# Attention steps of a two-layer fp32 trunk: loads issued one step ahead of their use, the samples' matmuls placed behind their step's scores

## The chip, the cores and the metric

One core of one Trainium2 chip runs the whole program. The metric is the device time of one execution in microseconds (us). The core has five engines that each run their own instructions in order: PE (TensorE: matmuls and transposes), DVE (VectorE), ACT (ScalarE), POOL (GpSimd) and SP (SyncE), which here only issues DMA transfers. An instruction that has to wait holds everything behind it on its own engine.

## The reference

One inference step of a trunk of two layers, each an attention and a gated feed-forward part with a causal convolution. It runs over 1024 prompt positions and over 8 samples of 16 new positions with caches, 1152 positions in all, with 1024 features, all in fp32. Layer 0 (mixer A) has 16 query heads on 4 key/value heads, a window of the own chunk of 64 and two before it, and a learned sink; layer 1 (mixer B) has 16 heads of keys and values shared from one projection, and a band of the own chunk and eight before it. Every part is conditioned (adaLN) by a vector c and closed by a LayerNorm of a scaled residual:

```python
ada = (sc @ w_ada[l] + b_ada[l])[:, None, :]          # sc = silu(c)
sh_m, sc_m, g_m, sh_f, sc_f, g_f = jnp.split(ada, 6, axis=-1)
h = x * (1 + sc_m) + sh_m
q = h @ w_q;  k, v = ...                              # layer 1: shared k_b, v_b
s = einsum(q, k) * ATTN_SCALE + bias;  s = where(valid, s, NEG_INF)
o = softmax(s, with sinks in layer 0) @ v
x = layer_norm(DEEPNORM_ALPHA * x + (1 + g_m) * (o @ w_o), ...)
h = x * (1 + sc_f) + sh_f
f = (gelu(conv(h @ w_up)[g]) * conv(h @ w_up)[a]) @ w_down
x = layer_norm(DEEPNORM_ALPHA * x + (1 + g_f) * f, ...)
```

## The kernel before, in words

The program runs an opening, tables, and then for each layer an attention, its output projection and a feed-forward part. An fp32 operand is split into a high part (a cast on ACT, L166) and a low part (a subtraction on POOL or DVE, L177), and a product takes three matmuls on the parts; `split` does both.

An attention is a loop of 64 steps: 8 groups of columns times 2 heads times 4 pairs of query tiles. A step issues the scores of its pair (`scores`: matmuls L548 and L551, then the softmax on DVE at L515 and ACT's exponential at L519). Around them the loop places, by tables that are indexed by the step number: the projection of later queries (`qload` and `qblock`, table QAT; PE L295), the row sums (`sums`, PE L624, a DMA at L627), the transposes of the weights of an earlier half (`weigh`: PE L576, the cast by ACT at L582, the subtraction by DVE at L583), the products with the values (`finish`: PE L598, ACT L611, DVE L612, POOL L636, the store to oN in DRAM at L638), and the samples' work (table ITEMS: `item_scores` L687, `item_weigh` L713 with its copies on DVE at L714 and L715, `item_values` L722 with DVE L730, `item_out` L735 with DVE L744). Towards the end of the loop the attention's outputs come back from oN and are split for the output projection (`oload`, table OAT, DMA L644, into H), the samples' outputs too (`sload`, SAT), and the first four tiles of the output projection's weights are loaded (`woload`, WAT, DMA L181). The output projection's matmuls are those at L308.

In the first attention there is also background work: `ada(1)` and `ada(2)` multiply c by 16 slabs of 512 KB of conditioning weights each. A slab is one DMA (L215), then four matmuls (L223), which the trace shows as eight. The loop calls `self.step(BGA)`, which moves this work on by 0.6 of a slab a step.

All of these loads of 512 KB (queries' weights, conditioning, outputs, output projection's weights) pass through `ws`, a ring of two staging slots: a load's DMA can go out when the slot's last reader is done, an ACT cast and a POOL subtraction, or PE for a slab of conditioning.

What stands where on an engine is set by a scheduler that walks the program and puts each instruction into its engine's order by a modelled time. `issue_after(m)` holds the instructions of its block behind instruction m on the same engine; it sets an order and makes nothing wait on another engine. Where `split` is called sets from when its cast may be put into ACT's order.

Of the kernel before, what the change touches and what calls it, by code (L numbers as in the profile page):

```python
# [102 lines left out]
class Trunk:  # L103
    def __init__(self, ctx, tc, I, O):
# [53 lines left out]
        self.items = []  # L158
# [20 lines left out]
    def wload(self, src, eh="a", el="p", dst=None):  # L179
# [3 lines left out]
        self.split(s, h, l, eh, el)  # L183
        self.step(self.bgrate)
        return h, l

# [19 lines left out]
    def ada(self, gi, bank, ring=None):  # L206
# [4 lines left out]
        lead = [None] * 4  # L211
        for k in range(8):
            for hf in range(2):
                w = ring.next()
                nc.sync.dma_start(w, self.I["adaw"][gi, k, hf])  # L215
                for j in range(4):
                    with ExitStack() as es:
                        if lead[j] is not None:
                            es.enter_context(self.tc.issue_after(lead[j]))
                        if j:  # L220
                            es.enter_context(self.tc.high_priority())
                            es.enter_context(self.tc.issue_after(first))
                        mm = nc.tensor.matmul(  # L223
                            ps[32 * j : 32 * j + 32, hf * 256 : hf * 256 + 256],
                            self.cT[:, k * 32 : k * 32 + 32],
                            w[:, j * 256 : j * 256 + 256],
                            start=k == 0 and hf == 0,
                            stop=k == 7 and hf == 1,
                            tile_position=(0, 32 * j),
                            skip_group_check=True,  # L230
                        )
                    first = mm.ins if j == 0 else first
                    lead[j] = lead[j] or mm.ins
                yield
# [140 lines left out]
    def attention(self, l, wk):  # L375
# [132 lines left out]
        def qload(c):  # L508
            qw[c] = self.wload(I[("wq0", "wq1")[l]][c])
# [1141 lines left out]
```

## Time and profile before

| | us |
|---|---|
| median of 3 runs | 2829.28 |
| lowest and highest | 2822.47, 2830.57 |
| profiled execution: its own time | 2830.02 |
| its span, first to last instruction | 2828.2 |
| PE busy | 2717.7 (96% of the span) |
| DVE busy | 1813.6 (64%) |
| ACT busy | 1294.3 (46%) |
| POOL busy | 1171.1 (41%) |
| mean granted TensorE clock | 0.986 |

Busy time of PE includes time at a lowered clock. The span less PE's busy time, 110.5 us, is the time in which PE did nothing. The first attention runs from about 105 to 395 us, the second from about 1545 to 1945 us; the feed-forward parts take most of the rest. In a row of waits stand the waiting line, what released it, the total in us, the number of times and the longest. In a row of windows stand the busy time (and the number of instructions) of each engine in the stretch, then the granted TensorE clock, the busy share of the DMA engines and their GB/s. In a row of the timeline stand the start and the duration in us, the engine, the line, the operation, the tiles, the shape and the number of like instructions taken together, and in brackets the idle time ahead of it with its releaser.

### The profile page before, as it was taken

To read this page: it belongs to the slowest core of one execution; us is meant where nothing else is said; L and a number is where in the kernel's file an instruction comes from. 1 tells how busy PE (TensorE), PEld (TensorE's weight loads), DVE (VectorE), ACT (ScalarE), POOL (GpSimd) and SP (SyncE) were. 2 spreads that over 40 slices of the span, in tenths; PEclk is the share of its full clock that TensorE was granted. 3 is DMA by queue.
4 is the path that set the end of the run, shared out by engine and by line. 5 is a ranking of instruction groups with operands and counts; after the bars stand their busy time and mean duration, and the time that the engine had idled before them with its cause. 6 is when DMAs were issued, how large, how long until landed. Compare 5 with 4: busy or idle time off the path is not lost. (4 is left out here: it accounts for less than half of the span.)

```text
span 2828.2 us, 47410 instructions
## 1 busy us (share of the span) xinstructions
PE 2717.7 (96%) x17734; PEld 2419.7 (86%) x17734; DVE 1813.6 (64%) x3673; ACT 1294.3 (46%) x2624; POOL 1171.1 (41%) x773
## 2 busy tenths in 40 slices
PE   7999999999999999999999899979999999999997
PEld 5887768989999998887999788857899999997886
DVE  4475768776666783565112767666787778874764
ACT  3475733433333443544325666662454444444442
POOL 2132433444443457664731121242454433358662
PEclk9999999999999999999999999999999999999999
DMA  8655444464444346664875457683532222247652
GB/s 296 217 159 178 124 150 163 150 234 144 145 146 152 134 148 219 231 216 163 289 243 186 115 142 194 173 254 105 174 122 80 74 74 78 71 138 250 211 198 80
DMA packets 214598, 468.00 MB, mean 165 GB/s; under 512 B 35456, under 2 KB 109904, under 8 KB 214368
## 3 DMA queue, kind: packets, MB, share of 16 engines
q1 hardware_dynamic: 214368, 464.98, 50.2%
q8 instruction: 139, 2.28, 0.3%
q14 instruction: 91, 0.75, 0.1%
HBM read 365.17 MB, written 109.17 MB: 168 GB/s over the span
## 5 line engine op out<-in xcount | busy, mean ns | idle before, releaser
L1227 PE MATMUL PS<-H,wh 128*128 128x256 f32 (+1 forms) x2560 | 395.9, 297 | 0.0
L1227 PEld LDWEIGHTS PS<-H,wh 128*128 128x128 f32 x2560 | 361.6, 191 | 0.4 <-issue 0.4
L1292 DVE TENSOR_TENSOR xa<-xa 128x384 fp32r<-128x384 f32 x132 | 182.5, 1393 | 222.9 <-ACT xa L166 221.3
L1189 DVE TENSOR_TENSOR F<-PS,F 128x192 f32<-128x192 f32 (+2 forms) x600 | 192.0, 350 | 180.0 <-PE PS L1227 176.9
L177 POOL TENSOR_TENSOR wl<-ws,wh 128x1024 fp32r<-128x1024 f32 x72 | 182.1, 2533 | 276.9 <-ACT wh L166 263.9
L295 PE MATMUL PS<-H,wh 128*128 128x384 f32 (+1 forms) x1536 | 294.7, 337 | 0.0
L166 ACT CAST wh<-F 128x512 fp32r<-128x512 f32 (+1 forms) x230 | 155.1, 681 | 296.2 <-PE PS L1227 150.5
L1066 DVE SCALAR_TENSOR_TENSOR F<-F 128x1024 f32<-128x1024 f32 x320 | 265.7, 871 | 4.8 <-ACT F L1105 3.4
L295 PEld LDWEIGHTS PS<-H,wh 128*128 128x128 f32 x1536 | 267.1, 188 | 1.4 <-issue 0.8
L1227 PE MATMUL PS<-H,wl 128*128 128x256 f32 (+1 forms) x1280 | 229.1, 299 | 9.2 <-ACT F L1194 5.1
L177 DVE TENSOR_TENSOR wl<-F,wh 128x512 fp32r<-128x512 f32 x198 | 197.9, 1007 | 44.2 <-ACT wh L166 43.6
L166 ACT CAST wh<-ws 128x512 fp32r<-128x512 f32 (+1 forms) x158 | 129.6, 825 | 207.7 <-PE PS L1227 89.7
L1299 PE MATMUL PS<-wh,xa 128*128 128x512 f32 x696 | 222.5, 396 | 0.0
L1227 PEld LDWEIGHTS PS<-H,wl 128*128 128x128 f32 x1280 | 189.9, 191 | 16.9 <-issue 6.2
L1227 PE MATMUL PS<-xa,wh 128*128 128x256 f32 (+1 forms) x1280 | 196.1, 295 | 0.5 <-DVE xa L177 0.5
L1227 PEld LDWEIGHTS PS<-xa,wh 128*128 128x128 f32 x1280 | 178.6, 188 | 1.3 <-DVE xa L177 0.9
L1075 POOL TENSOR_TENSOR F<-F 128x16 f32<-128x16 f32 x88 | 46.6, 530 | 312.4 <-DVE F L1066 230.6
L308 PE MATMUL PS<-wh,H 128*128 128x256 f32 (+1 forms) x936 | 171.0, 314 | 4.5 <-DVE X L364 3.0
L295 PE MATMUL PS<-H,wl 128*128 128x384 f32 (+1 forms) x768 | 154.7, 342 | 2.5 <-ACT H L166 2.1
L1299 PEld LDWEIGHTS PS<-wh,xa 128*128 128x128 f32 x696 | 130.6, 188 | 30.6
L166 ACT CAST xa<-xa 128x384 fp32r<-128x384 f32 x132 | 67.5, 513 | 186.5 <-DMA xa<-actD 186.4
L636 POOL TENSOR_TENSOR F<-F,X 64x512 f32<-64x512 f32 x62 | 80.3, 1295 | 171.1 <-DVE F L612 134.1
(255 smaller groups left out, 6119.9 us busy)
## 6 DMA issues: line engine op xcount, KB each, us to landing
F<-in_wdn_dram SPq DMA_DIRECT2D x72, 512.0 KB
ws<-in_adaw_dram SPq DMA_DIRECT2D x64, 512.0 KB
ws<-in_wdn_dram SPq DMA_DIRECT2D x60, 512.0 KB
actD<-F SPq DMA_DIRECT2D x44, 576.0 KB
xa<-actD SPq DMA_DIRECT2D x132, 192.0 KB
ws<-in_wup_dram SPq DMA_DIRECT2D x49, 512.0 KB
F<-in_adaw_dram SPq DMA_DIRECT2D x48, 512.0 KB
F<-in_wup_dram SPq DMA_DIRECT2D x39, 512.0 KB
```

The source lines that it names most:

```text
L166: nc.scalar.copy(out, in_)
L177: self.eng(el).tensor_sub(lo, src, hi.bitcast(F32))
L295: mm = self.nc.tensor.matmul(out[:, 0:n], w[a][:, k * 128 : k * 128 + 128], H[:, p, k, s0 : s0 + n], start=i == 0, stop=i == 23)
L308: self.nc.tensor.matmul(out[:, 0:n], H[:, p, j * kn + k, t0 : t0 + 128], w[a][:, k * n : k * n + n], start=i == 0, stop=i == 23,)
L636: self.eng("v" if last else "p").tensor_mul(on[r, q], on[r, q], rb[r, :])
L1066: nc.vector.scalar_tensor_tensor(o, u, cw[:, cc, i : i + 1], o, op0=ALU.mult, op1=ALU.add)
L1075: nc.gpsimd.tensor_add(y3[:, :, 0:2], y3[:, :, 0:2], E4[:, cc])
L1189: nc.vector.tensor_add(d, o, x)
L1227: self.pairmm = nc.tensor.matmul(ps[:, 0:m], w[a][:, k * 128 : k * 128 + 128], x(p, k, n), start=start and c == 0, stop=c == 11, skip_grou ...
L1292: nc.vector.tensor_sub(lo, raw, hi.bitcast(F32))
L1299: self.downmm = nc.tensor.matmul(ps, a[p][:, i * 128 : i * 128 + 128], w[q][:, hf * 512 : hf * 512 + 512], start=j == 0 and c == 0, stop=j ...
```

## The change

The loads of the two attentions are cut in two. The DMA is put out at one step, and the split (ACT's cast and the low part) goes on a list, `todo`, that is run just behind the scores of the next step, with its ACT part queued behind the last exponential of those scores (`amark`). This holds for the queries' weights from the second group on, the attention's outputs, the samples' outputs and the first four tiles of the output projection's weights. The queries' loads go out one step earlier (at step 8c-1), the last group's at 47 instead of 48; the outputs' loads one a step (steps 51 to 56, where two went out at 51 before), and the samples' outputs and the projection's weights one step later.

The conditioning of the first attention gets a ring of one slot of its own, `ws[1]`, and all other loads there have only `ws[0]` until it is done; then the ring of two is back. A slab's DMA goes out in one call of the generator and its matmuls come in the next, with the first of them queued behind the last score matmul so far (`pmark`). The rate BGA goes from 0.6 to 0.7 slabs a step.

Of the samples' work, the loads of a sample (`item_load`) are issued one sample ahead: the first ahead of the loop, the next behind the values of the one before. The PE part of each piece is queued behind the step's last score matmul.

The diff, cut to its core:

```diff
-BGA = 0.6
+BGA = 0.7
 BGF = 1.3
 QAT = {}
+for c in range(7):
+    QAT[max(0, 8 * c - 1)] = [(c + 1, None)]
 for c in range(5):
-    QAT[8 * c] = [(c + 1, None)]
     for j, k in enumerate((1, 3, 6)):
         QAT[8 * c + k] = [(c + 1, j)]
-QAT.update({40: [(6, None)], 41: [(6, 0)], 43: [(6, 1)], 46: [(6, 2)], 48: [(7, None), (7, 0)], 49: [(7, 1)], 50: [(7, 2)]})
-OAT = {51: (0, 1), 52: (2,), 53: (3,), 54: (4,), 55: (5,)}
-SAT = 56
-WAT = {57: 0, 58: 1, 59: 3, 60: 2}
+QAT.update({41: [(6, 0)], 43: [(6, 1)], 46: [(6, 2)], 48: [(7, 0)], 49: [(7, 1)], 50: [(7, 2)]})
+OAT = {51: 0, 52: 1, 53: 2, 54: 3, 55: 4, 56: 5}
+SAT = 57
+WAT = {58: 0, 59: 1, 60: 3, 61: 2}
...
-    def wload(self, src, eh="a", el="p", dst=None):
+    def wload(self, src, eh="a", el="p", dst=None, later=False):
         s = self.ws.next()
         self.nc.sync.dma_start(s, src)
         h, l = dst or self.wring.next()
-        self.split(s, h, l, eh, el)
+        self.after(lambda: self.split(s, h, l, eh, el), later)
         self.step(self.bgrate)
         return h, l
+
+    def after(self, f, later):
+        if later:
+            self.todo.append(f)
+        else:
+            f()
+
+    def run_todo(self):
+        todo, self.todo = self.todo, []
+        with self.tc.issue_after(self.amark):
+            for f in todo:
+                f()
...
-    def ada(self, gi, bank, ring=None):
+    def ada(self, gi, bank, ring=None, lag=False):
...
+        def mms(k, hf, w):
+            for j in range(4):
+                with ExitStack() as es:
...
+                    else:
+                        if lag:
+                            es.enter_context(self.tc.issue_after(self.pmark))
+                    mm = nc.tensor.matmul(
...
         for k in range(8):
             for hf in range(2):
                 w = ring.next()
                 nc.sync.dma_start(w, self.I["adaw"][gi, k, hf])
-                for j in range(4):
...
-                yield
+                if lag:
+                    yield
+                mms(k, hf, w)
+                if not lag:
+                    yield
...
-        def qload(c):
-            qw[c] = self.wload(I[("wq0", "wq1")[l]][c])
+        def qload(c, later=False):
+            qw[c] = self.wload(I[("wq0", "wq1")[l]][c], later=later)
...
-                    nc.tensor.matmul(o, q, klo[a][:, kc], start=False, stop=True, **kw)
+                    self.pmark = nc.tensor.matmul(o, q, klo[a][:, kc], start=False, stop=True, **kw).ins
...
-                softmax(pieces, p, n, self.sink[:, h : h + 1] if l == 0 else None, nm, L[:, i : i + 1])
+                self.amark = softmax(pieces, p, n, self.sink[:, h : h + 1] if l == 0 else None, nm, L[:, i : i + 1])
...
         def oload(c):
             s = self.ws.next()
             nc.sync.dma_start(s, self.oN[c])
-            self.split(s, self.H[:, 0, c, 0:1024], self.H[:, 1, c, 0:1024], "a", "p")
+            self.todo.append(lambda: self.split(s, self.H[:, 0, c, 0:1024], self.H[:, 1, c, 0:1024], "a", "p"))
...
         def item_scores(x):
-            item_load(x)
...
             nc.vector.tensor_scalar_mul(osm, ob[:, 0:128], x.rs)
+            k = 8 * p + s + 1
+            if k < 16:
+                item_load(xs[k])
...
+        narrow = self.ws
+        if self.bg:
+            self.ws = Ring(narrow.items[0:1])
...
+        item_load(xs[0])
         self.wo = {}
         steps = []
         for i, x in enumerate(work):
             scores(x)
+            self.run_todo()
             k = i // 2
...
                 if bi is None:
-                    qload(c)
+                    qload(c, True)
...
             if not self.bg and len(sbk.items) == 4:
                 sbk.items = [0, 1, 2, 3, 4]
+                self.ws = narrow
             for _ in range(ITEMS.count(i)):
                 steps += items.pop(0)
             for _ in range(min(len(steps), 1 + (len(steps) > 4) + (len(steps) > 8))):
-                steps.pop(0)()
-            for c in OAT.get(i, ()):
-                oload(c)
+                with self.tc.issue_after(self.pmark):
+                    steps.pop(0)()
+            if i in OAT:
+                oload(OAT[i])
             if i == SAT:
                 sload()
             if i in WAT:
-                self.woload(l, WAT[i])
-        assert not items
+                self.woload(l, WAT[i], True)
+        assert not items and self.ws is narrow
+        self.run_todo()
...
-        self.bg = [self.ada(1, 4), self.ada(2, 4)]
+        self.bg = [self.ada(g, 4, Ring(self.ws.items[1:2]), True) for g in (1, 2)]
```

Line numbers of the changed kernel are higher: L223 becomes L237, L548 L571, L551 L574, L576 L599, L598 L621, L624 L647, L687 L709, L713 L735, L722 L744, L735 L760, L308 L331, L166 L168, L519 L542, L582 L605, L611 L634. No instruction of PE is added or taken away in the three places that follow.

PE, in the first attention, at two places near the same step: slabs of conditioning (the rows with ws,C), scores (xa), transposes of weights (C,F) and products with values (X_70). Before:

```order
L223 MATMUL PS<-ws,C 32x256 x8
L548 MATMUL PS<-xa 128x256
L576 MATMUL PS<-C,F 128x128 x4
L551 MATMUL PS<-xa 128x256
L548 MATMUL PS<-xa 128x256
L551 MATMUL PS<-xa 128x256
L598 MATMUL PS<-X_70,xa 128x256 x6
L598 MATMUL PS<-X_70,xa 128x128 x2
L624 MATMUL PS<-C,F 4x128
```

and of the change:

```order
L237 MATMUL PS<-ws,C 32x256 x4
L571 MATMUL PS<-xa 128x256
L574 MATMUL PS<-xa 128x256
L599 MATMUL PS<-C,F 128x128 x4
L571 MATMUL PS<-xa 128x256
L574 MATMUL PS<-xa 128x256
L571 MATMUL PS<-xa 128x256
L574 MATMUL PS<-wl,xa 128x256
L621 MATMUL PS<-X_70,xa 128x256 x6
L621 MATMUL PS<-X_70,xa 128x128 x2
L647 MATMUL PS<-C,F 4x128
L237 MATMUL PS<-ws,C 32x256 x4
```

Before, matmuls of two slabs stand together (x8); now slabs stand singly, and from one to the next lie six score matmuls, four transposes, eight matmuls with values and one transpose of sums.

PE, late in the first attention: the products of a sample with its values (PS<-F), and the transpose of the result (PS<-C,F 128x128 in a row by itself), between which DVE has to scale the result. Before:

```order
L576 MATMUL PS<-C,F 128x128 x3
L548 MATMUL PS<-xa,H 128x256
L551 MATMUL PS<-wl,H 128x256
L722 MATMUL PS<-F 32x128 x8
L548 MATMUL PS<-xa,H 128x256
L551 MATMUL PS<-wl,H 128x256
L735 MATMUL PS<-C,F 128x128
L713 MATMUL PS<-C,F 128x128
L713 MATMUL PS<-C,F 16x128
```

and of the change:

```order
L571 MATMUL PS<-xa,H 128x256
L574 MATMUL PS<-wl,H 128x256
L744 MATMUL PS<-F 32x128 x8
L331 MATMUL PS<-wh,H 128x512 x2
L331 MATMUL PS<-wl,H 128x512 x2
L331 MATMUL PS<-wh,H 128x512 x2
L735 MATMUL PS<-C,F 128x128
L735 MATMUL PS<-C,F 16x128
L760 MATMUL PS<-C,F 128x128
L744 MATMUL PS<-F 32x128 x8
```

Before, two score matmuls stand between the values of a sample and the transpose of its result; now six matmuls of the output projection and the two transposes of the next sample stand there.

ACT, late in the second attention: the exponentials of a step (L519, L542), the casts of transposed weights (PS at L582, L605) and the casts of the outputs that came back (H<-ws). Before:

```order
L582 CAST X_70<-PS 128x512
L501 ACTIVATE H<-PS 64x384
L582 CAST wh<-PS 128x512
L582 CAST wl<-PS 128x512
L166 CAST H<-ws 128x1024 x2
L582 CAST wh<-PS 128x512
L519 ACTIVATE F<-F,C 128x384
L519 ACTIVATE F<-F,C 128x512
L519 ACTIVATE F<-F,C 128x640
```

and of the change:

```order
L542 ACTIVATE F<-F,C 128x128
L605 CAST X_70<-PS 128x512
L542 ACTIVATE F<-F,C 128x256
L168 CAST H<-ws 128x1024
L542 ACTIVATE F<-F,C 128x640
L542 ACTIVATE C<-C 128x272
L634 COPY F<-PS 64x512
L605 CAST wh<-PS 128x512
L605 CAST wl<-PS 128x512
L605 CAST wh<-PS 128x512
```

Before, two casts of outputs stand together ahead of the casts of transposed weights of the step and ahead of its exponentials; now one stands behind an exponential of the step.

More of the change, by code (lines that the diff above doesn't have):

```diff
@@ L157, in __init__ @@
         self.bgacc = 0
-        self.items = []
+        self.todo = []
+        self.pmark = None
     def bank(self, i):
@@ L215, in ada @@
                 nc.sync.dma_start(w, self.I["adaw"][gi, k, hf])
-                for j in range(4):
[L217 to L233, printed above, removed]
-                yield
+                if lag:
[3 more added lines that the diff above has]
+                    yield
         row = ring.next()
@@ L755, in item_out, with item @@
                 self.split(src, *hs, "a", "p" if l else "v")
-        def item(p, s):
+        xs = []
+        for k in range(16):
             x = Item()
-            x.p, x.s = p, s
+            x.p, x.s = divmod(k, 8)
+            xs.append(x)
+        def item(x):
             return [lambda f=f: f(x) for f in (item_scores, item_weigh, item_values, item_out)]
@@ L790, in attention @@
             qblock(1, 0, qw[1])
-        items = [item(p, s) for p in range(2) for s in range(8)]
+        items = [item(x) for x in xs]
+        item_load(xs[0])
         self.wo = {}
@@ L986, in residual, with woload @@
         return x
-    def woload(self, l, i):
+    def woload(self, l, i, later=False):
         X1, X2 = self.X1, self.X2
@@ L1257, in ffn @@
             if l == 0 and 3 <= j < 19:
-                with self.tc.issue_after(self.pairmm):
+                with self.tc.issue_after(self.pmark):
                     self.skew_b(j - 3)
```

23 lines of the change are left out of this document (19 added, 4 removed).

## The prediction

> **What bounds the kernel now.** I read the windows of the whole span first. In the feed-forward parts PE is busy all the time, and the order there is not touched; time can only come from the two attentions. Their windows (busy us of PE, PEld, DVE, ACT and POOL in each, then the granted clock of PE, the DMA share and GB/s):
>
> ```profile
> 150.00:200.00 50.00, 49.90 (x386) 46.19 (x384) 36.82 (x119) 35.62 (x106) 14.49 (x18) 1.00 0.46 145
> 200.00:250.00 50.00, 46.54 (x385) 37.49 (x383) 29.53 (x102) 27.15 (x82) 11.80 (x13) 0.93 0.64 190
> 250.00:300.00 50.00, 47.21 (x390) 38.91 (x383) 34.58 (x123) 30.65 (x94) 9.52 (x11) 0.93 0.44 138
> 300.00:350.00 50.00, 44.35 (x358) 34.38 (x357) 39.45 (x134) 36.26 (x100) 27.68 (x24) 0.90 0.44 135
> 350.00:400.00 50.00, 43.40 (x277) 31.06 (x276) 28.25 (x79) 22.40 (x51) 19.98 (x15) 0.90 0.50 151
> 1800.00:1850.00 50.00, 42.95 (x292) 37.44 (x294) 33.37 (x103) 33.01 (x73) 16.93 (x13) 0.93 0.63 184
> ```
>
> PE is the bound here too: no other engine is above 40 of 50 us. The loss has two parts: PE waiting (18.5 us from 200 to 400) and PE at a lower clock. The waits, first of the first attention (100 to 400 us), then of the second (1545 to 1960 us):
>
> ```profile
> PE PS L223 <- DMA ws<-in_adaw_dram: 6.6, 6, 2.3
> PE PS L735 <- DVE F L730: 2.8, 3, 1.9
> PE PS L722 <- DVE F L714: 1.6, 4, 0.5
> PE PS L687 <- DVE F L515: 0.6, 1, 0.6
> PE PS L713 <- DVE wh L583: 0.5, 1, 0.5
> ...
> PE PS L576 <- DVE wh L583: 10.4, 8, 5.4
> PE PS L713 <- ACT C L519: 2.4, 1, 2.4
> PE PS L308 <- ACT xa L166: 1.7, 1, 1.7
> ```
>
> The second part is seen in windows laid where the clock is low:
>
> ```profile
> 231.00:237.60 6.60, 6.45 (x35) 5.08 (x36) 3.56 (x10) 4.71 (x15) 2.36 (x1) 0.50 0.57 185
> 255.00:261.40 6.40, 6.40 (x48) 4.02 (x41) 2.50 (x12) 2.43 (x6) 0.59 (x1) 0.50 0.30 96
> 330.00:333.20 3.20, 3.12 (x23) 2.92 (x27) 1.81 (x9) 2.16 (x9) 3.20 (x2) 0.50 0.72 224
> 337.00:343.40 6.40, 6.38 (x43) 4.40 (x44) 4.51 (x19) 3.23 (x11) 2.96 (x2) 0.50 0.28 81
> 354.00:363.80 9.80, 9.19 (x50) 6.22 (x51) 5.64 (x22) 6.30 (x15) 5.91 (x3) 0.50 0.42 143
> 1842.00:1848.60 6.60, 4.07 (x18) 3.42 (x19) 3.94 (x9) 4.49 (x7) 3.01 (x4) 0.50 0.90 302
> ```
>
> Work done at half the clock costs half its busy time: 3.2 us each in the first two, 1.6, 3.2 and 4.6 in the next three (9.4 together), 2.0 in the last. The first two begin where two waits for conditioning slabs end (2.29 and 2.05 us, in the next but one fence), the last in the one long wait of the second attention. So a wait of 2 us or more costs about 3.2 us besides itself, and I use that as its price.
>
> **The long wait of the second attention.** The chain of waits and ACT's and PE's timelines there:
>
> ```profile
> 1836.95 5.11 DMA ws<-oN
> 1842.19 0.96 issue
> 1843.15 0.59 ACT wh L582
> ...
> 1842.09 1.04 ACT L166 CAST H<-ws 128x1024 fp32r<-128x1024 f32 x1 [3.18 <-DMA ws<-oN]
> 1843.15 0.58 ACT L582 CAST wh<-PS 128x512 fp32r<-128x512 f32 x1
> ...
> 1844.52 1.97 PE L576 MATMUL PS<-C,F 128*128 128x128 f32 x8 [5.40 <-DVE wh L583]
> ```
>
> An output's cast (L166) stands in ACT's order ahead of the casts of transposed weights (L582), its transfer takes 5.11 us, and all of ACT, then DVE, then PE waits for it. In the change a cast is reached one step later, behind that step's exponentials. Transfer and step are about equally long (a step there is some 5.7 us: the 64 steps fill about 365 of that attention's 400 us), so the cast should find its data. That takes away 5.4 us and 2.0 us of lower clock. What is late next: a cast of 1.04 us still stands ahead of some L582, eleven of them in all. Bounds: all eleven reach PE, +11; none does, and the 2.4 us wait of L713 on an exponential goes with the stall, −2.4. Nearest to the rows is that they mostly do not: the seven other waits of L576 in the row above are 5.0 us in all, over the whole of the attention. I take −0.6: **−8.0** for this part (−10 to +3.6).
>
> **The conditioning in the first attention.** Removed are its waits, 6.6 us, and the two stretches of lower clock, 6.4 us: −13.0. Added is what the single slot costs. PE's rows, then SP's:
>
> ```profile
> 212.88 0.64 PE L223 MATMUL PS<-ws,C 128*32 128x256 f32 x8
> 215.51 0.64 PE L223 MATMUL PS<-ws,C 128*32 128x256 f32 x8 [0.45 <-DMA ws<-in_adaw_dram]
> 217.16 0.64 PE L223 MATMUL PS<-ws,C 128*32 128x256 f32 x8
> 219.97 0.64 PE L223 MATMUL PS<-ws,C 128*32 128x256 f32 x8 [0.60 <-DMA ws<-in_adaw_dram]
> 231.15 1.08 PE L223 MATMUL PS<-ws,C 128*32 128x256 f32 x8 [2.29 <-DMA ws<-in_adaw_dram]
> 254.30 0.68 PE L223 MATMUL PS<-ws,C 128*32 128x256 f32 x8 [2.05 <-DMA ws<-in_adaw_dram]
> ...
> 213.58 2.96 SPq L215 DMA_DIRECT2D ws<-in_adaw_dram x2
> ```
>
> The slabs at 212.88 and 217.16 share a slot, as do those at 215.51 and 219.97; SP puts the next DMA out as soon as PE is done with a slab (213.58). From a slab's matmuls to those of the next in the same slot it takes 4.46 us where PE waited for it (219.97 less 215.51), and at most 4.28 us in the other case. With one slot, that is the least distance between any two slabs. How much work has PE between them? I counted the 31 intervals in the new order with start-to-start times such as these:
>
> ```profile
> 246.22 1.24 PE L598 MATMUL PS<-X,xa 128*128 128x256 f32 x9
> 249.13 0.66 PE L576 MATMUL PS<-C,F 128*128 128x128 f32 x4
> 250.52 0.28 PE L551 MATMUL PS<-wl,xa 128*128 128x256 f32 x1
> ```
>
> For the interval shown with the change: 0.57 for the slab, 0.9 for six score matmuls (0.12 to 0.2 each), 0.59 for four transposes (249.13 to 249.72), 1.0 for eight matmuls with values, 0.1 for the sums: 3.2 us, 1.3 short of 4.46. Of the 31, 15 are short, by 0.4 to 2.4 us and by some 15 us in all (12 if the distance is 4.2, 19 if the slab's own 0.57 does not count as work). Two come near or go above 2 us. For one of them I add a stretch of lower clock, 3.2; bounds are none and four, 0 to 12.8. So 15 + 3.2 − 13.0 = **+5.2**. Below, it goes to −13.0, if the scheduler's places leave PE enough other waits to cover the transfers; above, 19 + 12.8 − 13.0 = +18.8. SP, which issues everything in order, stands at each slab until PE has freed the slot, and behind it queue the loads of keys and of the sums' reciprocals and the stores to oN; that speaks against the lower end.
>
> On the clock the trace and the Trainium skill differ. Its page "TensorE: Matmul & The Clock Gate", section "Part 1: The HAM clock gate", has the clock fall to half after about one idle window of 3.4 us. Here it fell after waits of 2.29 and 2.05 us, so the measurement decides; by the page no new wait would be long enough, and this part would be +2.0.
>
> **The end of the first attention.** Samples' waits (L735, L722, L687, L713) are 5.5 us in the rows above, and the lower clock costs 9.4 us from 330 to 364. In the new order more work stands between a sample's values and the transpose of its result, which answers to L735's 2.8; but in other places the transposes of a sample's weights still stand right ahead of its values, as before, and L722 needs DVE's copies between. I take half of the waits, −2.8, and, as these stretches of low clock follow several short waits, half of their cost, −4.7: **−7.5**. Bounds: all of it, −14.9; on the other side the samples' work, held behind the scores, finishes later and PE has nothing to cover it with: as much again as now, +5.5.
>
> **The rest.** Queries' weights go out one step earlier, their casts one step later: PE had no wait on them in the first attention, so 0; the cover is the six steps between load and use. Projection's weights are cast one to two steps later; the wait at L308 for such a cast is 1.7 us in the second attention, and it can only grow: 0 to +4, the length of a transfer. I take +0.4. Samples' loads one sample ahead: PE shows no wait on them, 0.
>
> **Sum.** −8.0 + 5.2 − 7.5 + 0.4 = −9.9 from the profiled execution's 2830.0 us, which is 0.7 above the median: **2820 us**.
>
> **The rivals.**
>
> *The single slot decides (slower).* Every short interval becomes a wait, several fall close together and the clock goes down with them, +18.8; SP's standing delays the values' chain, so that the end gains nothing, 0; the second attention gains only its long wait, −7.4. 2830.0 + 11.4 = 2841. It decides from where a slab's round through its slot (4.46 us) is longer than PE's work to the next. For it: 15 of 31 intervals. Against it: PE had covered such waits in pairs before and can only lose what no other wait already takes.
>
> The Trainium skill warns of this in "TensorE: Matmul & The Clock Gate", section "HAM oscillation": where the compute for a tile is shorter than the wait for its DMA, PE is throttled at every tile. By that rule the rival would be right; the trace so far shows it for 2 of the 6 waits.
>
> *Nothing much (no change).* The output's cast only moves: its transfer shares SP and the DMA engines with the samples' loads (0.90 busy in the window from 1842), so it lands late again and stalls the exponentials instead; conditioning +5, end −5: 2830.
>
> *The large gain.* The scheduler's order lets slabs arrive in time, −13.0; the end loses most of its waits and its low clock, −10; second attention −8: 2799.
>
> **How the numbers follow.** Forecast 0.36 (own range 2812 to 2829), large gain 0.22, no change 0.14, slower 0.28. About 0.3%, 8.5 us, is what a measurement of this kernel can tell from no change. Six tenths of the forecast and all of the large gain are beyond it, 0.44; four tenths of the forecast and most of "nothing much", 0.27; slower, 0.29. The range runs from just above the large gain's extreme to just above the slower case: 2797 to 2845.
>
> **What would show it.** In the changed profile: no wait of L599 (L576 before) above 2 us near the outputs' casts, and the clock at 1.00 there; waits of L237 (L223 before) on its DMA at some 15 places and 10 to 20 us in all, with low clock behind the longest; waits of L760 and L744 (L735 and L722) halved, and fewer low stretches after 320 us; L331 (L308) waiting no longer than 2 us. I am wrong if slabs cost less than 5 us or more than 25, or if the end of either attention is longer than before.

## The result, and the profile after

The changed kernel takes 2863.58 us (median of 4, 2859.88 to 2867.72), the kernel before, on the same chip, 2829.93 (2822.47 to 2830.73): a ratio of 1.0124 (95% interval 1.0107 to 1.0141), some 35 us slower. The forecast was 2820, a little faster, with slower as a rival at 2841; the time lies above the range.

Windows laid from the first score matmul of an attention to the last matmul with values tell where. Before, first and second attention (columns as in the prediction's first fence):

```profile
105.60:391.30 285.70, 267.52 (x2077) 221.17 (x2075) 194.27 (x645) 178.63 (x511) 90.67 (x86) 0.94 0.49 152
1558.90:1937.70 378.80, 346.36 (x2444) 289.61 (x2444) 255.24 (x789) 234.22 (x540) 87.91 (x86) 0.98 0.58 166
```

and in the changed kernel:

```profile
104.90:415.40 310.50, 277.74 (x2085) 224.96 (x2083) 207.08 (x645) 180.30 (x515) 92.19 (x87) 0.93 0.45 141
1583.60:1973.10 389.50, 356.08 (x2444) 294.27 (x2444) 256.44 (x789) 235.38 (x540) 87.73 (x86) 0.96 0.58 161
```

The first attention is 24.8 us longer, the second 10.7; the span grew by 33.0 (2828.2 to 2861.2), so the rest of the program did not get longer. In the first, PE stands idle for 32.8 us (310.50 less 277.74) where it was 18.2. In the second PE's idle time is almost the same, 33.4 against 32.4, but the mean granted clock fell from 0.98 to 0.96: about 16 us of clock lost (0.04 of 389.5) against 8. The loss is not in one place. These are single executions; how far the clock alone moves such a window is in the last section.

PE's waits in the changed kernel, the first attention, then the second:

```profile
PE PS L237 <- DMA ws<-in_adaw_dram: 11.4, 11, 2.3
PE PS L571 <- DVE F L538: 8.1, 13, 1.7
PE PS L744 <- DVE F L635: 2.3, 2, 1.5
PE PS L621 <- DVE F L635: 2.2, 1, 2.2
PE PS L760 <- DVE F L752: 0.4, 1, 0.4
...
PE PS L331 <- ACT xa L168: 5.3, 2, 3.6
PE PS L744 <- DMA F<-in_cvB_dram: 4.3, 1, 4.3
PE PS L599 <- DVE wh L606: 4.2, 7, 1.5
PE PS L760 <- DVE C L752: 3.2, 2, 2.7
PE PS L318 <- POOL wl L179: 2.3, 3, 2.0
```

The waits for slabs (L237) grew from 6.6 to 11.4, less than the 15 that the forecast took. L760 (L735 before) is down from 2.8 to 0.4, as forecast. The 5.4 us wait of the second attention is gone: L599 waits 1.5 at most. But there are waits that the forecast had not seen: score matmuls of the first attention wait 8.1 us for DVE's softmax (L571 for L538, where the row of before, below, has 0.5), and L744 and L621 wait 4.5 us for DVE's L635; in the second there are waits for a sample's cached values, for L752 and for the output projection's weights.

```profile
PE PS L548 <- DVE F L515: 0.5, 2, 0.3
```

A cause of these waits for DVE shows in four lines of the timelines of POOL, DVE and PE, here for the wait of L621:

```profile
168.44 2.35 POOL L179 TENSOR_TENSOR wl<-ws,wh 128x1024 fp32r<-128x1024 f32 x1
168.63 2.18 DVE L644 TENSOR_TENSOR F<-F 128x4 f32<-128x4 f32 x1
170.73 0.68 DVE L635 TENSOR_TENSOR F<-PS,F 64x512 f32<-64x512 f32 x1
171.46 1.15 PE L621 MATMUL PS<-X,xa 128*128 128x256 f32 x8 [2.20 <-DVE F L635]
```

L644 adds the sinks to the row sums: 4 elements a partition, usually 0.16 us. Here it takes 2.18 us. It starts while POOL works on the low part of a queries' weight (L179), and ends when POOL does. Everything on DVE behind it is late by 2 us, and PE waits. Three more waits come right behind such an addition, DVE being busy without a break from it to the releaser: 1.47 and 1.66 us of L571 (at 112.40 and 320.05 us, behind additions of 2.25 and 3.15) and 1.46 us of L744 (at 376.96, behind one of 1.73). The four are 6.8 us. The rows of that addition over the whole run (minimum, median and maximum in ns), in the changed kernel and before:

```profile
L644 DVE TENSOR_TENSOR F<-F x32: 132/208/3152, 109.7 to 391.3; 128x4 f32<-128x4 f32 x32
...
L621 DVE TENSOR_TENSOR F<-F x32: 141/164/2286, 114.7 to 367.9; 128x4 f32<-128x4 f32 x32
...
L644 DVE TENSOR_TENSOR F<-F 128x4 f32<-128x4 f32 x32 | 24.3, 760 | 3.9 <-ACT F L643 3.8
L621 DVE TENSOR_TENSOR F<-F 128x4 f32<-128x4 f32 x32 | 13.7, 428 | 5.0 <-ACT F L620 4.6
```

Thirty-two additions of 0.16 us are 5 us; they take 24.3 in the changed kernel and 13.7 before. The change moved the splits of queries' weights to step 8c, right behind the scores, and an even step is where `sums` runs: low part and addition now meet more often. Theory H, below, is that this hold costs the first attention its time; theory S is the forecast's slower rival, the single slot.

### The profile page after: what moved, and what is told of

It is laid out like the page before. It is cut to its first block, busy times and chain, and to the rows that moved or that the text cites. A ratio compares the mean times of both kernels' runs of the same rounds, so it can differ in the third digit from the quotient of the medians.

```text
span 2861.2 us, 47400 instructions
## 1 busy us (share of the span) xinstructions
PE 2735.0 (96%) x17734; PEld 2427.4 (85%) x17734; DVE 1819.0 (64%) x3673; ACT 1295.1 (45%) x2624; POOL 1163.7 (41%) x773
## 5 line engine op out<-in xcount | busy, mean ns | idle before, releaser
L1329 DVE TENSOR_TENSOR xa<-xa 128x384 fp32r<-128x384 f32 x132 | 175.1, 1336 | 229.0 <-ACT xa L168 228.9
L168 ACT CAST wh<-F 128x512 fp32r<-128x512 f32 (+1 forms) x230 | 155.1, 681 | 298.8 <-PE PS L1264 150.1
L179 POOL TENSOR_TENSOR wl<-ws,wh 128x1024 fp32r<-128x1024 f32 x72 | 181.6, 2526 | 186.2 <-ACT wh L168 149.1
L179 DVE TENSOR_TENSOR wl<-F,wh 128x512 fp32r<-128x512 f32 x198 | 198.1, 1009 | 42.4 <-ACT wh L168 42.0
L168 ACT CAST wh<-ws 128x512 fp32r<-128x512 f32 (+1 forms) x158 | 129.5, 825 | 203.4 <-PE PS L1264 91.0
L331 PE MATMUL PS<-wh,H 128*128 128x256 f32 (+1 forms) x936 | 170.9, 314 | 7.5 <-DVE X L387 3.7
L331 PEld LDWEIGHTS PS<-wh,H 128*128 128x128 f32 x936 | 137.2, 196 | 17.9 <-DVE X L387 3.9
```

What stands on the lines that cost most here:

```text
L168: nc.scalar.copy(out, in_)
L179: self.eng(el).tensor_sub(lo, src, hi.bitcast(F32))
L331: self.nc.tensor.matmul(out[:, 0:n], H[:, p, j * kn + k, t0 : t0 + 128], w[a][:, k * n : k * n + n], start=i == 0, stop=i == 23,)
L1329: nc.vector.tensor_sub(lo, raw, hi.bitcast(F32))
```

## The experiments

**Three parts, alone and taken away.** The change falls into three parts that can be switched one by one: the slot (conditioning on one slot, a call late, BGA 0.7), the loads (splits behind the next step's scores, new tables for loads) and the samples (loads one sample ahead, matmuls behind the step's scores). With all three undone in the first attention, as in j3 below, the order there is that of before on every engine. Taking one part away from the changed kernel:

```diff
# e1: the slot
-BGA = 0.7
+BGA = 0.6
...
-        if self.bg:
-            self.ws = Ring(narrow.items[0:1])
...
-        self.bg = [self.ada(g, 4, Ring(self.ws.items[1:2]), True) for g in (1, 2)]
+        self.bg = [self.ada(1, 4), self.ada(2, 4)]
# e3: the samples; the loads one sample ahead go too
+            item_load(x)                      # in item_scores
...
-                with self.tc.issue_after(self.pmark):
-                    steps.pop(0)()
+                steps.pop(0)()
# e4: the loads, in wload; so too in oload and sload; QAT, OAT, SAT and WAT as before
-        self.after(lambda: self.split(s, h, l, eh, el), later)
+        self.split(s, h, l, eh, el)
```

> The change, with the conditioning of the first attention as it was before: two shared slots, a slab's matmuls in the same call as its DMA, 0.6 slabs a step. Theory S (the single slot is the loss): the 11.4 us of waits for slabs fall to about 6, and the low clock behind them goes with them, so the time falls by 15 to 25 us, to 2840 to 2848. Theory H (the low parts of the queries' weights now run on POOL just when DVE adds the sinks, and DVE is held until POOL is done): the waits of score matmuls on DVE (8.1 us) stay, and the time falls by at most 10 us, to 2854 or more.

> The change, with the samples' work as before: a sample's loads ahead of its own scores, and its matmuls not queued behind the step's scores. If the loads one sample ahead cost the second attention its 9 us (the new 4.3 us wait for cached values, the 2.7 us wait of L760), the second attention gets 5 to 9 us shorter: 2855 to 2859. If the later splits and loads of the output projection's weights cost it, no change there: 2861 to 2866.

> The change, with every split at its load again and the old tables for the loads of queries, outputs and weights. Theory H: POOL's low parts leave the sums' additions, first attention 8 to 15 us shorter; in the second the 3.6 us wait of the output projection goes, and the old 5.4 us wait for an output's cast comes back: 2848 to 2858. Theory S: first attention the same, total 2860 to 2868.

and each part alone, by two of these edits at a time:

> The kernel before with the conditioning's part of the change alone: one slot of its own, matmuls a call after their DMA, 0.7 slabs a step, other loads on one slot meanwhile. Theory S: the slab waits rise from 6.6 to about 11 us, with low clock behind them, 2836 to 2846. Theory H, in which the slot hurts only through what stands beside it: within 5 us of before, 2823 to 2833.

> The kernel before with the loads' part alone: splits behind the next step's scores, loads at the changed steps. Theory H: additions of the sinks at the sums held by POOL's low parts, 2 us each time, and waits of sample values for cached values in the second attention: 2838 to 2850. Theory S: 2825 to 2833, since the slot is not there.

> The kernel before with the samples' part alone: loads one sample ahead, matmuls behind the step's scores. The forecast's step: the waits for L730 and L714 halve and the low clock at the end of the first attention with them, 2818 to 2824. If the end of the attentions is bound by the transfers: 2825 to 2832.

| slot | loads | samples | ratio to before | 95% interval |
|---|---|---|---|---|
| x | | | 1.0023 | 1.0012 to 1.0035 |
| | x | | 1.0069 | 1.0054 to 1.0085 |
| | | x | 1.0015 | 1.0002 to 1.0029 |
| | x | x (e1) | 1.0097 | 1.0080 to 1.0114 |
| x | x | (e3) | 1.0117 | 1.0102 to 1.0133 |
| x | | x (e4) | 1.0054 | 1.0036 to 1.0072 |
| x | x | x | 1.0124 | 1.0107 to 1.0141 |

Alone, the parts add to 1.07%, together they cost 1.24%, and the loads are the largest, 20 us alone, 0.70% when taken from the whole. In the profiles they do not add up attention by attention: the first takes 285, 294 and 285 us with the slot, the loads and the samples alone, against 286 before and 310 with all three. The slot is 0.23% alone (6.5 us), and its slab waits by themselves are

```profile
PE PS L236 <- DMA ws<-in_adaw_dram: 8.6, 8, 2.8
```

so theory S falls as the main cause: it expected 2836 or more of f1, which took 2832.14, and 2840 to 2848 of e1, which took 2852.69 (short of theory H's 2854 too). e3 (2860.05) falls between its two expectations, short of what the samples' early loads would bring if they were to blame for the second attention. e4 (2841.37) and f2 (2847.74) show that it is the loads; theory H had e4 at 2848 at the least, so the loads do more than hold DVE. Where, show the two attentions of f2:

```profile
106.10:399.80 293.70, 271.35 (x2084) 218.39 (x2080) 198.14 (x645) 178.69 (x514) 94.61 (x89) 0.96 0.50 152
1565.90:1960.10 394.20, 359.48 (x2444) 296.80 (x2444) 256.39 (x789) 235.69 (x540) 87.77 (x86) 0.96 0.56 159
```

By itself the loads' part costs more in the second attention, 15 us in this profile, than in the first, 8; and the 32 additions take 16.8 us in it, hardly more than before. f3 (2834.17) misses both of its ranges on the slow side: the samples' part gains nothing.

**The hold.** Two runs move the split away from the sums or take the addition out (the prompt's outputs of layer 0 then leave out the sinks), and one does the latter in the kernel before, as a control:

```diff
# e2: queries' loads at 8c-2, so that the split falls into an odd step
-    QAT[max(0, 8 * c - 1)] = [(c + 1, None)]
+    QAT.setdefault(max(0, 8 * c - 2), []).append((c + 1, None))
...
# g1, and g0 on the kernel before
-                nc.vector.tensor_add(L[:, cs], L[:, cs], M[:, cs])
```

> The change, with the queries' loads one more step earlier (at step 8c-2), so that their split falls into an odd step, which has no sums. Theory H: the long additions at L644 (five of 2.2 to 3.2 us) shrink to their usual 0.2 us, the waits of score matmuls on DVE fall from 8.1 to below 3 us, and the time falls by 8 to 15 us, to 2849 to 2856. Theory S: no change beyond 3 us, 2861 to 2866.

> The changed kernel without the addition of the sinks to the prompt's row sums (L644, 32 small additions on DVE), so the prompt's outputs of layer 0 leave the sinks out. Theory H: with nothing on DVE to be held, score matmuls wait for DVE less than 3 us (8.1 us with it), and no DVE instruction of the sums is longer than 0.5 us: 10 to 16 us shorter than the change, 2847 to 2853. Theory S: at most 5 us shorter, 2858 or more; 32 additions of 0.16 us are 5 us of DVE, which PE does not wait for. If the reciprocal behind is held instead, nothing is gained.

> Control for the run without additions: the kernel before without the addition of the sinks to the prompt's row sums (L621), so the prompt's outputs of layer 0 leave the sinks out. Theory H (what costs is POOL holding the addition): before has only three holds above 1.4 us and PE hardly waits behind them, so at most 5 us are gained, 2821 to 2828. If the additions cost by being there at all: 12 to 16 us are gained, 2810 to 2814, as from the change.

e2 gives 1.0089 (1.0074 to 1.0104), 0.35% better than the change, within what was expected in time, but not by the whole mechanism: the longest addition is still 2.35 us and L571 waits 6.7 us. g1 gives 1.0065 (1.0040 to 1.0090), 0.59% better than the change, and its slab waits and softmax waits both shrink:

```profile
PE PS L237 <- DMA ws<-in_adaw_dram: 4.8, 9, 1.1
PE PS L571 <- DVE F L538: 4.0, 8, 1.6
```

The control g0 gives 0.9997 (0.9984 to 1.0011). So leaving out the same 32 additions gains nothing in the kernel before and some 17 us in the changed one (8 to 25 by the two intervals). That is not the hold's size alone: with the addition gone the scheduler lays out the first attention anew in both kernels, and the shorter slab waits of g1 may belong to that.

Which operands are held? In h2 the sinks' exponential goes to PSUM, so that the addition reads one operand there; h3 is the same edit on the kernel before.

```diff
-                nc.scalar.activation(M[:, cs], M[:, cs], AF.Exp, bias=self.sinkH[:, hh : hh + 1])
-                nc.vector.tensor_add(L[:, cs], L[:, cs], M[:, cs])
+                t = self.bank(tbk.next())
+                e4 = t[:, 256:260]
+                nc.scalar.activation(e4, M[:, cs], AF.Exp, bias=self.sinkH[:, hh : hh + 1])
+                nc.vector.tensor_add(L[:, cs], L[:, cs], e4)
...
-            t = self.bank(tbk.next())
+            if l:
+                t = self.bank(tbk.next())
```

> The changed kernel with the exponential of the sinks written to PSUM, so that DVE's addition at the sums (L644) reads one operand from PSUM and one from SBUF; everything is computed. If POOL holds DVE only where both operands come from SBUF (no score softmax, which reads PSUM and SBUF, was ever held): no addition longer than 0.5 us, 10 to 17 us shorter, 2844 to 2852. If the hold is on any DVE access to SBUF: the holds of 2 us stay, 2858 to 2864.

> The kernel before with the same move of the sinks' exponential to PSUM. Theory H: three holds above 1.4 us and some of 0.6 to 1 us go, 0 to 6 us shorter than before, 2820 to 2827. If the operand's place does not matter: 2825 to 2832.

The same addition in h2:

```profile
L646 DVE TENSOR_TENSOR F<-F,PS x32: 136/154/161, 108.9 to 389.9; 128x4 f32<-128x4 f32 x32
```

Not one of 32 is above 0.161 us, though 18 of them meet a POOL instruction of 1.3 to 2.4 us: with one operand in PSUM DVE is not held. h2 takes 1.0056 (1.0034 to 1.0078), 0.68% better than the change. This is what the Trainium skill states in "SBUF — State Buffer", section "Who interferes with whom": a DVE instruction with two SBUF inputs contends with a GpSimd instruction that reads SBUF, and the ports that they share are an exclusive lock, so that the order in which they start decides which of them is blocked. The rows agree: the addition that started second took 2.18 us, to the end of a POOL instruction of 2.35, and the edit that the rule suggests took the hold away. As stated the rule is wider than the rows: a POOL instruction that reads one tile of SBUF did not hold an addition (last section). h3 missed: on the kernel before, the same edit costs 0.69% (1.0042 to 1.0096), and PE's order in the first attention is another one (the bank is taken earlier); its slab waits are

```profile
PE PS L223 <- DMA ws<-in_adaw_dram: 9.8, 9, 2.0
```

against 6.6. So h2's gain, like g1's, mixes the hold with such a shift. What speaks for the hold beside them: in e1, e2, e3 and e4 the 32 additions, all of them still there, take 14.6, 16.3, 18.0 and 15.2 us, and the first attention 296, 298, 303 and 296 us, against 24.3 and 310 in the change (one profile each). Taking any of the three parts away takes most of the extra holds away, so they come from the three together. That the hold costs the first attention time is shown; how much, between the 6.8 us of waits right behind it and some 17, is not.

**The second attention.** First the changed kernel with only the old tables for outputs and weights:

```diff
-OAT = {51: 0, 52: 1, 53: 2, 54: 3, 55: 4, 56: 5}
-SAT = 57
-WAT = {58: 0, 59: 1, 60: 3, 61: 2}
+OAT = {51: (0, 1), 52: (2,), 53: (3,), 54: (4,), 55: (5,)}
+SAT = 56
+WAT = {57: 0, 58: 1, 59: 3, 60: 2}
```

> The changed kernel with the old tables for the loads of outputs, samples' outputs and output projection's weights (steps 51 to 60), the splits still behind the next step's scores. Theory of the later steps: the second attention's loss comes from the loads being issued one step later, and it falls by 5 to 9 us there, 2852 to 2857. Theory of the held slot: it comes from a slot that is kept one step longer by the later split, so that the next load on SP waits; then no more than 3 us: 2858 to 2864.

1.0139 (1.0116 to 1.0163), or 2868.27 us, above both expectations: no gain, so the later steps are not what costs. Then four kernels whose first attention has the order of before, and whose second has one piece of the loads' part each (tables that differ by layer, and `later` only where named):

```diff
# j1: new tables          j2: old tables          j3: old tables          j4: new QAT only
# j2 and j4:
+                    qload(c, l == 1)
# j2 and j3, so too for the samples' outputs; j2 also woload(..., l == 1)
+            self.after(lambda: self.split(s, ...), l == 1)
```

> The first attention as before; in the second, every load at the changed kernel's steps, but each split at its load, as before. Theory of the later steps: it carries the second attention's loss of 8 to 13 us, 2834 to 2840. Theory of the held slot (a split one step later keeps a staging slot one step longer, and SP, which issues in order, stands before the next load): at most 4 us, 2824 to 2831.

> The first attention as before; in the second, every load at its old step, but each split behind the next step's scores. Theory of the held slot: 8 to 13 us longer than before, 2834 to 2840. Theory of the later steps: at most 4 us, 2824 to 2831.

> The first attention as before; in the second, only the splits of the attention's outputs go behind the next step's scores, loads at their old steps. This is the step of the forecast by itself: the 5.4 us wait behind an output's cast goes and 2 us of low clock with it, 2818 to 2822, if nothing takes its place. If the transfers bound that stretch and the wait moves to the samples' cached values: 2825 to 2832.

> The first attention as before; in the second, only the queries' weights changed: loads one step earlier, splits behind the next step's scores. If their casts, now behind the exponentials, come too late for the projection (waits of L318 on POOL's low part of 2 to 3 us in the change): 3 to 6 us longer than before, 2830 to 2834. If the queries' part is harmless here: 2825 to 2829.

In j2 the last group's weights are loaded and used at one step (48), so that its first block of queries is projected with weights that are not yet split: that one of 24 blocks is computed from the wrong data and does not wait for its weights; its matmuls are the same in number and shape. j1 takes 1.0007 (0.9993 to 1.0021) and j3 1.0007 (0.9993 to 1.0020): neither the steps nor the outputs' later splits cost or gain. j4 takes 1.0042 (1.0029 to 1.0056) and j2, which has the same piece, 1.0049 (1.0036 to 1.0062). The later split of the queries' weights carries it: j1 loads them at the same steps and splits them at once. How, shows in ACT's, POOL's and PE's timelines of the changed kernel:

```profile
1795.06 1.03 ACT L168 CAST wh<-ws 128x1024 fp32r<-128x1024 f32 x1
...
1798.74 0.14 POOL L551 MEMSET F<- 64x64 f32 x1 [8.12 <-DVE wl L606]
1798.88 2.35 POOL L179 TENSOR_TENSOR wl<-ws,wh 128x1024 fp32r<-128x1024 f32 x1
...
1798.19 0.66 PE L599 MATMUL PS<-C,F 128*128 128x128 f32 x4 [1.52 <-DVE wh L606]
1801.28 1.01 PE L318 MATMUL PS<-H,wl 128*128 128x384 f32 x2 [1.96 <-POOL wl L179]
...
1801.00:1804.40 3.40, 3.12 (x11) 3.02 (x12) 0.60 (x1) 0.59 (x1) 1.65 (x3) 0.50 0.59 175
```

The cast comes at 1795.06, between exponentials and the casts of transposed weights, and PE waits 1.52 us behind it. The low part could start at 1796.1, but on POOL a small MEMSET of the next head's bias stands ahead, which waits until 1798.74. PE's projection, one step behind the split, waits 1.96 us, and the clock goes to half for 3.4 us. In j4 it is the same, there with the bias's transfer as what the MEMSET waits for:

```profile
1771.42 0.14 POOL L560 MEMSET F<- 64x64 f32 x1 [8.76 <-DMA F<-skb]
1771.57 2.34 POOL L188 TENSOR_TENSOR wl<-ws,wh 128x1024 fp32r<-128x1024 f32 x1
...
1773.96 0.97 PE L327 MATMUL PS<-H,wl 128*128 128x384 f32 x2 [2.60 <-POOL wl L188]
```

In the changed kernel this place accounts for some 5 us (1.52 and 1.96, and half of 3.12 at the low clock), in j4 its two waits are 1.54 and 2.60. The rest of j4's 12 us is not put down to a place. Its second attention takes 393.1 us at a clock of 0.95, PE idles 35.7 us in it (32.4 before), and after 1840 us its long waits are others than before (5.01, 3.14 and 2.69 us for 5.40, 2.40 and 2.09). That last stretch is crowded with transfers. In the changed kernel a step of the chain of waits there and two windows:

```profile
1889.49 9.38 DMA F<-in_cvB_dram
...
1890.00:1895.00 5.00, 4.07 (x31) 2.83 (x23) 1.97 (x9) 1.36 (x6) 2.39 (x1) 1.00 1.05 246
1895.00:1900.00 5.00, 1.00 (x16) 0.65 (x16) 1.46 (x3) 3.34 (x7) 2.41 (x2) 0.66 1.11 355
```

The DMA engines' share is at its top there, 1.05 and 1.11 by the profile's measure, and a sample's cached values take 9.38 us. Which matmul waits longest there differs from kernel to kernel. j3, the forecast's step by itself, shows it: the 5.4 us wait is gone, and the window of its second attention is

```profile
1551.10:1935.50 384.40, 355.04 (x2444) 295.38 (x2444) 256.25 (x789) 233.76 (x540) 87.50 (x86) 0.96 0.58 163
```

PE idles 29.4 us, 3.0 less than before, and the clock is 0.96 instead of 0.98 in this execution. After 1840 us the longest waits are now 2.99 and 2.52 us. Whether these cost the clock is not shown, since equal programs differ as much (last section); over its ten runs j3 gains nothing.

**Both mended.** h2's edit and the queries' weights split at their load, in the second attention (k1) or in both (k2):

```diff
-                    qload(c, True)
+                    qload(c, l == 0)   # k1; k2: qload(c)
```

> The changed kernel with two things mended: the sinks' exponential in PSUM (as in h2_psum_after), and in the second attention the queries' weights split at their load. If the two causes found, POOL's hold on the sums' additions (about 0.7% of before) and the late split of the queries' weights in the second attention (about 0.4%), make up the change's loss and add up: 0.1 to 0.3% above before, 2829 to 2836. If the second attention's loss needs only the queries' weights together with something else of the change: 0.4% or more above before, 2838 or more.

> As k1_both_mended, with the queries' weights split at their load in the first attention too, still one step earlier. If the late split also costs the first attention something beside the hold: faster than k1_both_mended, 2822 to 2830, and perhaps faster than before. If not: as k1_both_mended within 3 us.

Both take 1.0059 (1.0043 to 1.0075, and 1.0042 to 1.0077), as h2 did: what cost j4 0.42% by itself gives nothing back here. It is also as long as e4 (1.0054), the changed kernel without the loads' part. So within these intervals h2's edit, its new order included, takes back all that the loads cost on top of the slot and the samples, and what is left is no more than what those two cost together. PE's waits in k1, first attention, then second:

```profile
PE PS L237 <- DMA ws<-in_adaw_dram: 10.4, 11, 2.1
...
PE PS L747 <- DMA F<-in_cvB_dram: 8.9, 2, 4.5
PE PS L599 <- DVE X L606: 6.0, 3, 4.6
```

The late low part is gone, and waits for cached values (8.9 where they were 4.3) and for transposed weights (4.6 in one) are there in its place. What is left lies in both attentions (296 and 386 us in k1's profile, 286 and 379 in that of before). So the second attention's loss is not settled as one cause: the queries' weights bring it by themselves, and why mending them gains nothing in the changed kernel stays open. No version that was run is shown to be faster than the kernel before.

## Why the prediction was wrong

By parts, the forecast gave the loads −7.6 us (−8.0 and +0.4), the slot +5.2 and the samples −7.5. Alone they cost 19.5, 6.5 and 4.2 us (0.69, 0.23 and 0.15%).

**The rest: queries' weights at 0.** This is the step that failed. It priced the move of the queries' casts by whether PE had waited for the weights in the first attention, and found cover in the steps between load and use. It did not ask what runs beside the low part on POOL at its new place, nor look at the second attention. In the second, the later split costs 12 us by itself (j4 against j1), with a low part that comes behind a waiting MEMSET and too late for the projection. In the first, the runs showed DVE's additions held by the low part, together with the other two parts: 24.3 us of additions where they were 13.7, at least 6.8 us of PE's waits, and 17 us gained without the additions, a new order included. A sign of it was in the profile of before, in a row that I had not read:

```profile
123.95 1.93 DVE L621 TENSOR_TENSOR F<-F 128x4 f32<-128x4 f32 x1
```

Before, PE had other work at 124 us and did not wait; that work made this hold free there.

The projection's weights, at +0.4 with +4 as the bound, came out near the bound in the profile after: L331 waits 5.3 us for such casts in the second attention, L308 waited 1.7. In e1, with the same loads, it is 1.7 again.

**The conditioning, +5.2.** Right in size, 6.5 us alone (0.12 to 0.35%), but in part by luck: the slab waits were to rise from 6.6 to 15 and came to 8.6 alone and 11.4 with the rest, at 8 and 11 places rather than 15. Where the 6.5 us lie, f1's profile does not show: its first attention is no longer than before (285 us, at a clock of 0.98 against 0.94).

**The long wait of the second attention, −8.0.** The wait went, as said. That nothing would take its place was wrong: in j3 alone other waits came up, PE's idle time fell by 3.0 us, and the time did not fall (1.0007). What was probably missing is the DMA engines' share there as a bound; no run had fewer transfers there to test it. In the kernel before, around the old wait:

```profile
1835.00:1840.00 5.00, 3.50 (x32) 2.11 (x31) 2.78 (x8) 3.28 (x10) 2.27 (x2) 1.00 0.98 244
1840.00:1845.00 5.00, 0.48 (x3) 0.48 (x3) 1.23 (x2) 2.12 (x3) 2.93 (x2) 0.70 1.02 353
```

The share is as high in the changed kernel around the new waits, and in j3 removing the wait behind one transfer showed the next (2.52 us for a sample's keys). The rival "nothing much" had this mechanism, for this part, and should have carried it.

**The end of the first attention, −7.5.** L735's wait fell from 2.8 to 0.4 as forecast, yet the samples' part alone is 0.15% slower (0.02 to 0.29). In f3 score matmuls wait 4.9 us for DVE's softmax, where they waited 0.5: waits came back at other lines.

**The price of a wait, 3.2 us of clock behind 2 us.** It held in kind: low clock stood behind the wait of 1.96 us above, and with those of 2.7 and 3.6 us:

```profile
1923.90:1927.30 3.40, 3.21 (x10) 2.53 (x11) 2.19 (x6) 0.83 (x2) 2.18 (x3) 0.50 0.60 188
1937.50:1944.30 6.80, 3.81 (x9) 3.07 (x10) 3.92 (x13) 4.60 (x9) 0.00 (x0) 0.50 0.73 238
```

Half of the busy time is 1.6 to 1.9 us each, nearer to the 2.0 of the old long wait than to 3.2. What was underrated is the total: the mean granted clock was 0.979 to 0.981 in the four runs of the changed kernel and 0.981 to 0.990, 0.985 in the mean, in the 81 of the kernel before that were taken beside the experiments; 0.005 of the span is some 14 us. The slower rival had its sign right, but mostly for a wrong cause: at 2841 it stopped short of 2863.58, and the slot alone gives 2832.14.

## What to carry to other kernels

Before moving a split, cast or subtraction, look at what the engine beside it does at the new place, not only at who waits for the result: here a POOL subtraction of 2.35 us held a DVE addition of 0.16 us to its end: in the changed kernel's profile, all 16 additions that began during a POOL instruction on two tiles of SBUF. Where transfers fill the DMA engines, removing one wait can move PE to the next, as in j3; look for DMA share to spare in the windows before counting on the gain. And judge parts of a change by switching them one by one, on a version that reproduces the old order with all switches off: profiles of the same order differed by several us, mostly through the clock.

## What the runs showed of the hardware that I had not expected

A held DVE instruction can miss its turn between two POOL instructions that follow each other. In h1, DVE's and POOL's timelines and PE's:

```profile
350.24 5.63 DVE L726 TENSOR_TENSOR C<-C 128x1 f32<-128x1 f32 x1
...
350.00 1.26 POOL L659 TENSOR_TENSOR F<-F,X 64x512 f32<-64x512 f32 x1 [2.32 <-DVE F L635]
351.22 4.64 POOL L179 TENSOR_TENSOR H<-ws,H 128x1024 fp32r<-128x1024 f32 x2
...
356.13 1.24 PE L744 MATMUL PS<-F 128*32 128x128 f32 x16 [6.25 <-DVE F L736]
```

One addition of a single element a partition waits for three POOL instructions in a row, 5.63 us, and PE for 6.25. It is not always so. In the kernel before, an addition was let in at the end of the first of two POOL subtractions:

```profile
310.62 2.29 DVE L621 TENSOR_TENSOR F<-F 128x4 f32<-128x4 f32 x1 [1.34 <-ACT F L620]
...
310.52 4.70 POOL L177 TENSOR_TENSOR H<-ws,H 128x1024 fp32r<-128x1024 f32 x2 [7.58 <-issue]
```

What decides between the two, the runs do not show. Nor does every POOL instruction hold: in e2 an addition began at 215.70 us, inside a POOL TENSOR_SCALAR on one tile of SBUF (L269, 215.19 us, 0.85 us long), and took its 0.16 us.

The clock made equal orders differ. j3's first attention has the instructions and the order of before; its window from the first score to the last values is

```profile
105.70:384.60 278.90, 260.63 (x2077) 216.21 (x2076) 195.00 (x645) 178.83 (x511) 90.45 (x86) 0.97 0.51 155
```

against 285.70 us at 0.94 in the profile of before, with PE's idle time the same (18.3 and 18.2 us).
